# Zeros in place of half-depth score products, in a float32 kernel of one block and two hybrid layers

## The chip, the cores and the metric

One core of a Trainium2 chip runs the whole kernel. The metric is the time on the device in microseconds; smaller is better. The kernel is one program with its instructions unrolled (39424 of them), on TensorE (PE, its weight loads shown as PEld), VectorE (DVE), ScalarE (ACT), GpSimd (POOL) and SyncE (SP), which issues the transfers.

## The reference

All is float32, 256 latent tokens and 256 context tokens, width 1024. A first block on the latent tokens alone, then two layers on both:

```
first block:  proj = rms_norm(x) @ w_in
  a: 8 query heads of 64 on 2 key/value heads; rms_norm and rotation of q, k
     out_a = softmax(q k^T / 8) v
  b: 8 heads of 64; rms_norm of q, k; three dilated windows, mixed by their
     softmax denominators (here one bias per head and pair of tokens)
  x += [rms_norm(out_a), rms_norm(out_b)] @ w_out
  x += conv_ffn(rms_norm(x))
layer l = 0, 1:  h = rmsnorm(x) * (1 + scale) + shift, latent and context
  attention: 8 heads, each with 2 components c of 64; keys: latent and context
     s_c = q_c k_c^T / 8;  p_c = softmax(s_c);  o = (p_0 - lam * p_1) v
  state space part (32 heads of 64, 8 groups, both directions), gates, merge, MLP
out = rmsnorm(x)
```

The context's own outputs are wanted in layer 0 only, so layer 1 has 256 query tokens and layer 0 has 512. The key products of a head's component contract over 64 numbers, and the array has 128 rows.

## The kernel before, in words

**Products.** Most products of the kernel are made of three: an operand is split into a high part (rounded by a copy to float32r, on ACT) and a low part (the rest, on DVE), and high x high, high x low, low x high are summed in PSUM. Weights come in 1 MB loads on SP into three `raw` buffers and are split there (`wload`, L118; `wsplit`, L127). All PE work goes through `mmul` (L315) and `transpose` (L309), so nearly all of it has line L316 or L311 in the profile and is told apart by tile names.

**Order.** While `self.pin` is set, PE keeps the order in which the program emits its instructions. Order on DVE, ACT, POOL and SP is the planner's, from its own costs. A `Stream` (L90) is a generator of products whose work is put out a few columns at a time between the stages of an attention.

**First block (`block1`, L387).** `products` (L486) makes q and k of four heads token-major; `turn4` (L496) transposes them on PE into a PSUM tile `ptq` and ACT copies them to `Tqa`, `Tqb`, `Tka`, `Tkb` (L504 without, L506 with a scale). Each such tile holds two heads on its two halves of 64 partitions; `Tka` has each of its two heads twice (L543). `scores` (L557) takes one head: its 64 partitions of q and of k, one float32 product for each of two query tiles, which the profile shows as two passes each: four of 256 columns per head, 16 heads. Softmax follows on DVE and ACT, `turn` transposes, `weigh` multiplies with v. At each of 18 steps the stream puts products between these three stages. The context `xc` is loaded at L766, after the first block's attention in the program, and is used from `mix_h(0, xc, 1, ...)` (L818) on; the tile itself is allocated for the whole first block.

**Layers (`attention`, L1014).** `qk_g` (L1065) makes q and k of a head h ahead of its scores. For each component c, `qhl[c]` holds q's high part on c's own half of the partitions and its low part on the other; `khh[c]` holds k's high part on both halves; `klo` holds k's low parts, component c's on its own half. A score unit is one head and a group of query tiles (128 tokens each): groups [0], [1], [2, 3] in layer 0 and [0], [1] in layer 1 (L1114). For each component and tile, `scores` (L1117) runs two float32r products into one PSUM region: all 128 rows of `qhl[c]` with `khh[c]` (high x high and low x high at once), then the 64 rows of c's half with `klo` (L1133). Groups of one tile have 512 columns (all keys), the group [2, 3] 256. Between the stages of a unit the stream puts 4096 columns of other products, those of the next head's q, k, v, or gates (`fill_g`, which borrows the tiles tagged khh, klo and qhl at the end).

Of the kernel before, what the change touches and what calls it, by code (L numbers as in the profile page):

```python
# [22 lines left out]
P = 128  # L23
# [40 lines left out]
# a head's columns with the pairs of the rotation in its two halves  # L64
ROPE1 = np.arange(64).reshape(2, 2, 16).transpose(1, 0, 2).reshape(-1)

# how the first products' operands are cut into loads
CUTS = [slice(a, b) for a, b in ((0, 2), (2, 4), (4, 6), (6, 8))]
# columns of products (in 256) between the stages of the first attention
B1_STEP = [7] * 12 + [2.8] * 6  # L70
# the rows of a product at which a stage that waits for the tensor engine comes in
FL = (4, 6)
# steps of the first up products before the norm's sums, and between these and their use
U0, U1 = 6, 4
# the row of the norm's output behind which the up products' next work is put
AF_K = 5
# the first pieces of the first layer's modulation come under the attention, the next ones at these up products
NADA = 4
ADA_UP = (8, 10, 12, 15, 18)
# when the stages of dt's part come in the attention  # L80
DT_STEP = (1, 3, 4, 5, 6, 7, 8)
# independent products between the heads of the attention and between the groups of the state space part, by layer
# [7 lines left out]
class Stream:  # L90
    """Products emitted a few at a time among other work."""
# [13 lines left out]
class Build:  # L105
# [35 lines left out]
    def wloadB(self, src, pool, bufs):  # L141
        """wload for mmB: all 256 columns in one tile"""
        nc = self.nc
        raw = self.wraw.tile([P, 8, 256], F32, tag="raw", name="raw")
        nc.sync.dma_start(raw, src)
        hi = pool.tile([P, 8, 256], F32R, tag="whB", name="whB", bufs=bufs)
        lo = pool.tile([P, 8, 256], F32R, tag="wlB", name="wlB", bufs=bufs)
        for ks in (slice(0, 4), slice(4, 8)):
            self.split(hi[:, ks], lo[:, ks], raw[:, ks])
        return hi, lo  # L150
# [12 lines left out]
    def mm2_g(self, outs, w, x, tok, k0=0, start=True, stop=True):  # L163
        """two products, row by row, in one bank or two"""
# [19 lines left out]
    def mmH_g(self, out, w, m, x, segs, **kw):  # L184
        """mmA, one accumulation per token segment"""
        for t in segs:
            yield from self.mmA_g(out[:, t], w, m, x, t, **kw)
# [40 lines left out]
    def fnorm(self, src, kts, n, dim, pool):  # L228
        """rstd of the mean over features, on all partitions (PSUM): src(k) is [P, n]."""
# [11 lines left out]
    def rstd(self, accs, n, dim, pool, between=None):  # L241
        """1 / sqrt(column sums of all of accs [P, n] / dim + eps), on all partitions (PSUM)"""
# [15 lines left out]
        # Newton's y (3 - v y^2) / 2 without the factors of 2: y grows by -2, 16, -8192  # L258
# [30 lines left out]
    # ------------------------------------------------------------------  # L289
# [30 lines left out]
    # ------------------------------------------------------------------  # L320
# [28 lines left out]
    def ada_g(self, l, j, pool, psum, pend=None, raws=()):  # L349
        """Columns 512 j .. 512 j + 511 of layer l."""  # L350
# [27 lines left out]
    def modcoef(self, l, which, g, col):  # L378
        """g * (1 + scale), for modulation `which` (scale tiles), stream col."""
# [6 lines left out]
    # ------------------------------------------------------------------  # L386
    def block1(self, xl, xc):  # L387
# [4 lines left out]
        with ExitStack() as es:  # L392
# [7 lines left out]
            # the first products' operands come in two halves of the rows  # L400
# [7 lines left out]
            # one start for the bank: it clears what tells the first products from the later ones in all of it  # L408
# [13 lines left out]
            # 1 / rms of each token: kept aside, for it cancels out in the norms of the heads but for their eps  # L422
# [7 lines left out]
            # rope tables times gains  # L430
# [16 lines left out]
            qT = {nm: wa.tile([P, n, S], F32, name="T" + nm) for nm, n in (("qa", 4), ("qb", 4), ("kb", 4), ("ka", 2))}  # L447
# [9 lines left out]
            def b4(ap, n):  # L457
                """[P, t, 64] for n heads"""
                return ap.rearrange("p t (o d) -> p t o d", o=1).broadcast_to([P, 2, n, ap.shape[2]])

            def h64(ap):
                """[P, t, h] for 64 columns"""
# [3 lines left out]
            def hstat(ps, n):  # L466
                """1 / rms of the heads of token-major products [P, t, n, 64], over that of the token"""
# [28 lines left out]
            def turn4(y, dst, scale=None):  # L496
                """token-major [P, t, 256] to [P, i, tokens]"""
# [5 lines left out]
                if scale is None:  # L503
                    nc.scalar.copy(dst, p3)  # L504
                else:
                    nc.scalar.activation(out=dst, in_=p3, func=AF.Identity, scale=scale)  # L506
# [3 lines left out]
            def qk_g(ci, nm, q):  # L510
# [12 lines left out]
                def later():  # L523
                    turn4(y.rearrange("p t h d -> p t (h d)"), qT[nm][:, 2 * q:2 * q + 2, :],
                          None if nm == "qa" else self.v1(nm + "c"))
# [10 lines left out]
            def kv():  # L536
# [9 lines left out]
                pend.append(lambda: turn4(yd.rearrange("p t b i d -> p t (b i d)"), qT["ka"]))  # L546

            # mixed = [norm(a), norm(b)]
# [8 lines left out]
            def scores(grp, h):  # L557
                j, rows = h // 2, slice(64 * (h % 2), 64 * (h % 2) + 64)
                q_, k_ = (qT["qa"][rows, j, :], qT["ka"][rows, h // 4, :]) if grp == "a" else (qT["qb"][rows, j, :], qT["kb"][rows, j, :])
# [187 lines left out]
            # the first two chunks start before the norm, which is made good after their products  # L747
# [13 lines left out]
        # conv ffn  # L761
# [80 lines left out]
    # ------------------------------------------------------------------  # L842
    def modulated(self, wk, x, t0, A, B, hi, lo):
        """hi/lo[:, k, t0:t0 + 256] = rmsnorm(x) * A + B"""
# [16 lines left out]
    def settle(self, x2, c, accs, tile, xa=None, A=None):  # L861
        """the squares of two new residual tiles, summed, and the tiles times A"""
# [22 lines left out]
    def apply(self, xa, r, B, h, t0):  # L885
        """h[:, k, t0:t0 + 256] = xa * r + B, split"""
# [8 lines left out]
    def mmdt_g(self, out, w, x, t):  # L895
        """64 columns of products: w's high and low parts side by side, their products on the two halves of the partitions"""
# [10 lines left out]
    def lead_w(self, l, w):  # L907
        """the weights of dt's products"""
# [5 lines left out]
    def lead(self, l, h, accs, xa, ads, wd):  # L914
        """the norm ahead of layer l on the latent tokens, with the context's part of the first products meanwhile"""
# [32 lines left out]
    def dt_g(self, l, ps, rows, lat_only):  # L948
        """the step sizes, token-major, and what hangs on them alone; rows: bias and log of a on all partitions"""
# [16 lines left out]
        # softplus: max(v, 0) + log(1 + exp(-|v|)), the logarithm as 2 artanh(e / (2 + e))  # L966
# [41 lines left out]
        if lat_only:  # L1008
            # only the states that leave the context are asked for: its first chunk's weights reach to its end
# [3 lines left out]
    # ------------------------------------------------------------------  # L1013
    def attention(self, l, hx, NQ, psd, psk, psq, wq):  # L1014
# [4 lines left out]
        with ExitStack() as es:  # L1019
            wk = es.enter_context(self.pool("att", reuse="tile"))  # L1020
            # lambda
# [33 lines left out]
            def v_g(p, t2s):  # L1055
                """V of heads 2 p, 2 p + 1, token-major"""
# [8 lines left out]
            def qk_g(h):  # L1065
                w = self.wload(a["w_qk"][l, h]) if h else wq
                # per component c: q as its high and low parts on the two halves of the partitions (high on c's
                # own half), k's high part on both halves, k's low part on c's own half
                khh = [wk.tile([P, 512], F32R, tag=f"khh{c}", name="khh", bufs=2) for c in range(2)]
                klo = wk.tile([P, 512], F32R, tag="klo", name="klo", bufs=2)  # L1070
                qhl = [wk.tile([P, NQ], F32R, tag=f"qhl{c}", name="qhl", bufs=2) for c in range(2)]

                def put_k(src, t):
                    for c in range(2):
                        for o in (c, 1 - c):
                            nc.scalar.copy(khh[c][half(o), t], src[half(c)])
                        nc.vector.tensor_tensor(out=klo[half(c), t], in0=src[half(c)], in1=khh[c][half(c), t].bitcast(F32), op=SUB)
# [27 lines left out]
            def products():  # L1105
# [4 lines left out]
                for job, tags in zip(PLAN[l][0], 3 * (("khh0", "khh1"), ("klo", "qhl0"))):  # L1110
# [6 lines left out]
            def scores(h, us):  # L1117
# [8 lines left out]
                for c in range(2):  # L1126
# [3 lines left out]
                    for i, u in enumerate(us):  # L1130
                        o, qs, kt = ps[:, i * kw:(i + 1) * kw], slice(u * 128, (u + 1) * 128), slice(512 - kw, 512)
                        self.mmul(o, qhl[c][:, qs], khh[c][:, kt], start=True, stop=False)
                        self.mmul(o, qhl[c][half(c), qs], klo[half(c), kt], start=False, stop=True)  # L1133
# [102 lines left out]
    # ------------------------------------------------------------------  # L1236
    def att_out_g(self, l, hx, att, NQ, c, wk, saved):
        """2 sigmoid(ga) * (att @ w_attn_o), columns 256 c .. 256 c + 255, to DRAM"""
# [22 lines left out]
    def rows(self, d, c, m, NQ):  # L1261
        """what one tile of 512 columns holds of chunk c in DRAM"""
# [5 lines left out]
    def gate_g(self, l, g, hx, NQ, c, wk, tags, ths, dst):  # L1268
        """2 sigmoid - 1 of columns 256 c .. 256 c + 255 of gate g"""
# [15 lines left out]
    def fill_g(self, l, jobs, hx, att, NQ, wk, tags=("th", "th")):  # L1285
        """products that do not hang on the work around them"""
# [6 lines left out]
    # ------------------------------------------------------------------  # L1293
    def ssd(self, l, hx, NQ, att):
# [6 lines left out]
        with ExitStack() as es:  # L1301
# [5 lines left out]
            def conv(ps, n, ti, dst):  # L1307
                """half of the 5-tap convolution + bias, then silu; n tokens in segments of 256"""
# [52 lines left out]
            def products(g, us):  # L1361
# [4 lines left out]
                if g == 7:  # L1366
                    # the merge's first products, as far as ys has come
# [6 lines left out]
            for g in range(8):  # L1374
# [8 lines left out]
                # token-major B and x  # L1383
# [30 lines left out]
                # states entering each chunk  # L1414
# [28 lines left out]
                def decay(c):  # L1443
                    """the weights of chunk c's tokens on its outputs, and of the state entering it"""
# [7 lines left out]
                    # forward decay below the diagonal, backward above it: the other exponent is 0 there  # L1452
# [18 lines left out]
                def output(c, E, R):  # L1471
                    """outputs of chunk c: [P, j, tokens]; those of two chunks in one bank where there are no others"""
# [61 lines left out]
                if g == 7:  # L1534
                    # more of them for the time in which the last ys come
# [24 lines left out]
    def so_g(self, l, ys, NQ, c, i, ps=None):  # L1560
        """ys @ w_ssd_o, columns 256 c .. 256 c + 255, second half of the rows first: PSUM tiles, products"""
# [15 lines left out]
    # ------------------------------------------------------------------  # L1577
    def merge_mlp(self, l, hx, ys, NQ, xsrc, es_x, es_op):
        """returns the new residual tiles"""
# [8 lines left out]
        with ExitStack() as es:  # L1588
# [89 lines left out]
            if last:  # L1678
                # the shift as one more token (two columns of it), to be added after the products
# [14 lines left out]
        with ExitStack() as es:  # L1694
# [4 lines left out]
            def hidden(j, t, u):  # L1699
                """the squares of u, split: tokens t of hidden tile j"""  # L1700
# [291 lines left out]
```

## Time and profile before

| | |
|---|---|
| three runs | 2402.43 us median (2401.62 to 2403.8) |
| profiled execution: span from its first to its last instruction | 2398.5 us |
| its time beside the span | not given on the page; the median of the runs is 3.9 us above the span |
| mean granted clock of PE | 0.997 |
| busy: PE, DVE, ACT, POOL | 2346.9, 1755.9, 1336.2, 38.4 us |
| chain that ended last | PE 85%, DVE 7%, ACT 5%, DMA 2% |
| first block's attention | about 36 to 128 us |
| attention of layer 0, of layer 1 | about 395 to 640 us, 1640 to 1820 us |

How to read it: a busy share is the union of an engine's instructions. PE's instructions overlap, each lasting longer than the distance to the next, so the distance between starts, not the duration, is what a product takes of the time. In the rows below, `64*128` is the part of the array in rows and columns, `64x512` the moving operand.

### The profile page before, as it was taken

Reading aid. Unit: us, or ns where it says so; the run is one execution under the profiler, and the core shown is the slowest. Engines: PE = TensorE matmul, PEld = TensorE weight load, DVE = VectorE, ACT = ScalarE, POOL = GpSimd, SP = SyncE. Lnnn points to the kernel's source line nnn. Section 1 sums busy time; section 2 is a strip of 40 time slices with the busy share of each in tenths; the row PEclk is TensorE's granted clock in tenths of the full one; section 3 lists DMA queues with packets and bytes.
Section 4 is the critical chain, followed back from the end, with each engine's and each line's share of the span. In section 5 each row is a group of like instructions: output and inputs, shape, how many; then the busy total and the mean of one; then the engine's idle time right before and its main releaser. Section 6 shows DMA issues by size and latency. Waiting matters only on the chain.

```text
span 2398.5 us, 39424 instructions
## 1 busy us (share of the span) xinstructions
PE 2346.9 (98%) x15516; PEld 2027.1 (85%) x15516; DVE 1755.9 (73%) x3562; ACT 1336.2 (56%) x2657; POOL 38.4 (2%) x32
## 2 busy tenths in 40 slices
PE   8999999999999999999999999999999999999998
PEld 7789998787778887778898878798888888899998
DVE  6578766776588878997574334387877999977776
ACT  5556545666466556874334232246776676755553
POOL 1000000000000000000000000000000000000000
PEclk9999999999999999999999999999999999999999
DMA  7546674121334434336334453353224444365553
GB/s 287 174 163 255 225 255 151 56 71 36 112 103 137 132 116 136 116 117 224 110 124 158 158 222 129 123 180 127 91 78 156 137 150 148 113 219 180 186 183 106
DMA packets 75032, 356.57 MB, mean 149 GB/s; under 512 B 9184, under 2 KB 16352, under 8 KB 38368
## 3 DMA queue, kind: packets, MB, share of 16 engines
q1 hardware_dynamic: 71088, 349.31, 42.0%
q10 hardware_dynamic: 3760, 4.75, 0.6%
q8 instruction: 122, 2.00, 0.3%
q14 instruction: 62, 0.51, 0.1%
HBM read 340.15 MB, written 13.89 MB: 148 GB/s over the span
## 4 chain that ended last, share of the span: by engine, by line
PE 85%; DVE 7%; ACT 5%; DMA 2%; issue 1%; SPq 0%; POOL 0%; DVEq 0%; ACTq 0%
PE psm L316 22%; PE psxs L316 6%; PE psso L316 5%; PE psu L316 5%; PE psz L316 4%; PE psk L316 3%; PE psv L316 3%; PE pss L316 3%; PE psga L316 3%; PE psd L316 3%; PE psgs L316 2%; PE pso L316 2%; PE psao L316 2%; PE psB L316 2%; PE psy L316 2%; PE psq L316 2%
## 5 line engine op out<-in xcount | busy, mean ns | idle before, releaser
L136 ACT CAST whi<-raw 128x1024 fp32r<-128x1024 f32 (+1 forms) x430 | 445.3, 1043 | 555.1 <-PE psm L316 263.8
L137 DVE TENSOR_TENSOR wlo<-raw,whi 128x1024 fp32r<-128x1024 f32 (+1 forms) x430 | 522.0, 1218 | 217.4 <-ACT whi L136 212.9
L316 PE MATMUL psm<-dh,whi 128*128 128x256 f32 (+1 forms) x576 | 182.4, 317 | 0.5 <-DVE x L1755 0.5
L316 PE MATMUL psm<-dl,whi 128*128 128x256 f32 (+1 forms) x576 | 182.2, 316 | 0.0
L316 PE MATMUL psm<-dh,wlo 128*128 128x256 f32 (+1 forms) x576 | 182.1, 316 | 0.0
L316 PE MATMUL psm<-hhi,whi 128*128 128x258 f32 (+2 forms) x544 | 179.5, 330 | 1.7 <-ACT whi L136 1.2
L316 PE MATMUL psm<-hlo,whi 128*128 128x258 f32 (+2 forms) x544 | 179.0, 329 | 0.4 <-DVE hlo L893 0.3
L316 PE MATMUL psm<-hhi,wlo 128*128 128x258 f32 (+2 forms) x544 | 178.1, 327 | 0.8 <-DVE wlo L137 0.8
L1456 ACT ACTIVATE E<-R,cstok 128x128 f32<-128x128 f32 x384 | 120.1, 391 | 37.4 <-PE psy L316 28.8
L316 PEld LDWEIGHTS psm<-dh,whi 128*128 128x128 f32 x576 | 108.7, 189 | 9.4 <-issue 1.9
L316 PEld LDWEIGHTS psm<-hhi,whi 128*128 128x128 f32 x544 | 103.1, 190 | 15.1 <-issue 2.9
L316 PEld LDWEIGHTS psm<-dl,whi 128*128 128x128 f32 x576 | 108.6, 189 | 7.4
L316 PEld LDWEIGHTS psm<-dh,wlo 128*128 128x128 f32 x576 | 108.6, 189 | 7.3
L316 PE MATMUL psxs<-hhi,whi 128*128 128x512 f32 x256 | 113.1, 442 | 0.0
L1755 DVE SCALAR_TENSOR_TENSOR x<-psm,mod,x 128x256 f32<-128x256 f32 x96 | 44.1, 481 | 92.2 <-PE psm L316 92.1
L316 PEld LDWEIGHTS psm<-hhi,wlo 128*128 128x128 f32 x544 | 103.2, 190 | 9.8 <-DVE wlo L137 1.2
L316 PEld LDWEIGHTS psm<-hlo,whi 128*128 128x128 f32 x544 | 103.2, 190 | 9.3 <-DVE hlo L893 1.2
L316 PE MATMUL psxs<-hhi,wlo 128*128 128x512 f32 x256 | 100.3, 392 | 0.0
L316 PE MATMUL psxs<-hlo,whi 128*128 128x512 f32 x256 | 100.3, 392 | 0.0
L1317 DVE SCALAR_TENSOR_TENSOR xT<-psxs,halfw,xT 128x510 f32<-128x510 f32 (+1 forms) x128 | 94.5, 741 | 0.5 <-ACT xT L1313 0.2
L1137 ACT ACTIVATE pr<-pss,mx 128x512 f32<-128x512 f32 (+1 forms) x96 | 58.5, 614 | 60.4 <-DVE mx L1135 58.6
L316 PE MATMUL psu<-hhi,whi 128*128 128x256 f32 x320 | 91.6, 286 | 0.5 <-ACT hhi L774 0.5
(470 smaller groups left out, 6985.2 us busy)
## 6 DMA issues: line engine op xcount, KB each, us to landing
raw<-in_w_m SPq DMA_DIRECT2D x68, 1024.0 KB, 4.9
araw<-in_ada SPq DMA_DIRECT2D x48, 1024.0 KB, 5.0
R<-csd SPq DMA_DIRECT2D x48, 512.0 KB, 6.2
raw<-in_w_up SPq DMA_DIRECT2D x22, 1024.0 KB, 5.0
raw<-in_w_qk SPq DMA_DIRECT2D x16, 1024.0 KB, 4.9
raw<-in_w_bc SPq DMA_DIRECT2D x16, 1024.0 KB, 5.1
raw<-in_w_xs SPq DMA_DIRECT2D x16, 1024.0 KB, 4.9
raw<-in_w_z SPq DMA_DIRECT2D x16, 1024.0 KB, 5.0
```

The lines of the kernel that those rows point to most:

```text
L136: nc.scalar.copy(h, r)
L137: nc.vector.tensor_tensor(out=lo[:, :nk, :n], in0=r, in1=h.bitcast(F32), op=SUB)
L316: i = self.nc.tensor.matmul(*args, **kw)
L1137: nc.scalar.activation(out=pt_[:, i * kw:(i + 1) * kw], in_=ps[:, i * kw:(i + 1) * kw], func=AF.Exp, scale=0.125, bias=mx[:, i:i + 1], acc ...
L1317: nc.vector.scalar_tensor_tensor(out=y[:, :, lo:hi], in0=u[:, :, lo + o:hi + o], scalar=wj(j), in1=y[:, :, lo:hi], op0=MUL, op1=ADD)
L1456: nc.scalar.activation(out=E[:, d, h, :], in_=R[:, d, h, :], func=AF.Relu, scale=-1.0, bias=self.cs_tok[:, c, i:i + 1])
L1755: nc.vector.scalar_tensor_tensor(out=xs[col][:, k, :], in0=ps[:, t], scalar=self.mod[l][:, 40 + k, col:col + 1], in1=xs[col][:, k, :], op0 ...
```

## The change

All score products become 128 rows deep. In the layers `klo` becomes a tile for each component, whose other half is set to zero on POOL for every head (two memsets of 64x512), and the second product uses all of `qhl[c]` with it: q's part on the other half meets zeros. In the first block the transposed keys get a tile for each half, `Tka0`, `Tka1` and, for b, the two halves of `xc`; the other 64 partitions of each are set to zero once (four memsets), and `turn4` copies each half of the partitions by an instruction of its own. q keeps its tiles. The number of products and their columns stay as they were. The rest of the diff takes out comments.

```diff
-            qT = {nm: wa.tile([P, n, S], ...) for nm, n in (("qa", 4), ("qb", 4), ("kb", 4), ("ka", 2))}
+            qT = {nm: wa.tile([P, n, S], ...) for nm, n in (("qa", 4), ("qb", 4))}
+            kT = {"ka": [wa.tile([P, 2, S], F32, name=f"Tka{i}") for i in range(2)], "kb": [xc[:, 4 * i:4 * i + 4, :] for i in range(2)]}
+            hrow = [slice(0, 64), slice(64, 128)]
+            for ts in kT.values():
+                for i in range(2):
+                    nc.gpsimd.memset(ts[i][hrow[1 - i]], 0.0)
...
-            def turn4(y, dst, scale=None):
+            def turn4(y, dsts, scale=None):
...
+                for rows, dst in dsts:
+                    if scale is None:
+                        nc.scalar.copy(dst[rows], p3[rows])
+                    else:
+                        nc.scalar.activation(out=dst[rows], in_=p3[rows], func=AF.Identity, scale=scale[rows])
...
+                    js = slice(2 * q, 2 * q + 2)
+                    dsts = [(slice(0, P), qT[nm][:, js, :])] if nm in qT else [(hrow[i], kT[nm][i][:, js, :]) for i in range(2)]
...
-                j, rows = h // 2, slice(64 * (h % 2), 64 * (h % 2) + 64)
-                q_, k_ = (qT["qa"][rows, j, :], qT["ka"][rows, h // 4, :]) if grp == "a" else (qT["qb"][rows, j, :], qT["kb"][rows, j, :])
+                j, i = h // 2, h % 2
+                q_, k_ = (qT["qa"][:, j, :], kT["ka"][i][:, h // 4, :]) if grp == "a" else (qT["qb"][:, j, :], kT["kb"][i][:, j, :])
...
-                klo = wk.tile([P, 512], F32R, tag="klo", name="klo", bufs=2)
+                klo = [wk.tile([P, 512], F32R, tag=f"klo{c}", name="klo", bufs=2) for c in range(2)]
+                for c in range(2):
+                    nc.gpsimd.memset(klo[c][half(1 - c)].bitcast(F32), 0.0)
...
-                        self.mmul(o, qhl[c][half(c), qs], klo[half(c), kt], start=False, stop=True)
+                        self.mmul(o, qhl[c][:, qs], klo[c][:, kt], start=False, stop=True)
```

## Rows read from the trace of the kernel before

**Rows 1.** The page: its head, and busy time, share and count of PE.
```profile
span 2398.5 us, 39424 instructions
...
PE 2346.9 (98%) x15516; PEld 2027.1 (85%) x15516; DVE 1755.9 (73%) x3562; ACT 1336.2 (56%) x2657; POOL 38.4 (2%) x32
```

**Rows 2.** Stretches of the two layers' attentions: length, then busy time by engine, clock.
```profile
395.00:640.00 245.00, 240.98 (x1310) 192.00 (x1309) 172.20 (x447) 159.04 (x412) 0.00 (x0) 1.00 0.20 69
1640.00:1820.00 180.00, 180.00 (x1209) 156.37 (x1208) 141.46 (x375) 127.71 (x297) 0.00 (x0) 1.00 0.28 99
```

**Rows 3.** Waits of PE, 395 to 645 us: total, times, longest.
```profile
PE pto L311 <- DVE o L1180: 1.4, 1, 1.4
...
PE pto L311 <- DVE dk L1005: 0.4, 1, 0.4
```

**Rows 4.** Timeline of PE, layer 0, one-tile unit: start us, duration us, instruction.
```profile
581.16 0.39 PE L316 MATMUL psgs<-hhi,wlo 128*128 128x512 f32 x1
581.40 0.40 PE L316 MATMUL pss<-khh,qhl 128*128 128x512 f32 x1
581.72 0.49 PE L316 MATMUL pss<-klo,qhl 64*128 64x512 f32 x1
582.14 0.50 PE L316 MATMUL pss<-khh,qhl 128*128 128x512 f32 x1
...
583.34 0.40 PE L316 MATMUL psgs<-hlo,whi 128*128 128x512 f32 x1
583.57 0.39 PE L316 MATMUL psgs<-hhi,wlo 128*128 128x512 f32 x1
```

**Rows 5.** Groups by line and form, PEld: count, busy us, mean ns, idle before.
```profile
L316 PEld LDWEIGHTS psgs<-hlo,whi 128*128 128x128 f32 x128 | 24.3, 190 | 2.8 <-issue 0.7
```

**Rows 6.** Timeline of PE, layer 0, a unit of two tiles.
```profile
599.75 0.40 PE L316 MATMUL psgs<-hhi,wlo 128*128 128x512 f32 x1
...
602.94 0.39 PE L316 MATMUL psgs<-hhi,wlo 128*128 128x512 f32 x1
```

**Rows 7.** Timeline of PE, layer 1, around a unit.
```profile
1788.77 0.28 PE L316 MATMUL psga<-hhi,wlo 128*128 128x256 f32 x1
...
1790.72 0.28 PE L316 MATMUL psga<-hlo,whi 128*128 128x256 f32 x1
1790.84 0.28 PE L316 MATMUL psga<-hhi,wlo 128*128 128x256 f32 x1
```

**Rows 8.** Timeline of PE, first block, one head.
```profile
43.19 0.28 PE L316 MATMUL psqk<-whB,hlo 128*128 128x256 f32 x1
43.40 1.13 PE L316 MATMUL pss<-Tka,Tqa 64*128 64x256 f32 x4
...
44.68 0.28 PE L316 MATMUL psqk<-wlB,hhi 128*128 128x256 f32 x1
```

**Rows 9.** Timeline of PE, state space part, float32 passes of 128 rows.
```profile
693.08 0.59 PE L316 MATMUL psst<-xw,Bt 128*128 128x256 f32 x2
...
693.75 0.40 PE L316 MATMUL psz<-hlo,whi 128*128 128x512 f32 x1
```

**Rows 10.** Timeline of POOL: the first row and one of the state space part.
```profile
0.24 0.10 POOL L1983 MEMSET const-float32-0.0<- 128x1 f32 x1 [0.24 <-issue]
...
728.46 1.42 POOL L1541 TENSOR_TENSOR ssq<-y 128x512 f32<-128x512 f32 x1 [709.48 <-DVE y L1539]
```

**Rows 11.** Tile Tkb: its copy (ns min/median/max, first and last start), its waiters.
```profile
L506 ACT ACTIVATE Tkb<-ptq,vb x2: 687/687/687, 80.2 to 112.2; 128x512 f32<-128x512 f32 x2
...
  PE pss L316: 1.6, 2
```

**Rows 12.** Tile xc: its load's issue, its first reader, landing of its transfers.
```profile
L766 SPq DMA_DIRECT2D xc<-in_ctx x1: 1133/1133/1133, 44.3 to 44.3; - x1
...
L234 ACT ACTIVATE sqa<-xc x1: 421/421/421, 168.3 to 168.3; 128x256 f32<-128x256 f32 x1
...
DMA to landing us min/median/max: 7.9/8.4/8.9
```

More of the change, by code (lines that the diff above doesn't have):

```diff
@@ L446, in block1 @@
                 tabs[nm] = (gc, gs)
-            qT = {nm: wa.tile([P, n, S], F32, name="T" + nm) for nm, n in (("qa", 4), ("qb", 4), ("kb", 4), ("ka", 2))}
+            qT = {nm: wa.tile([P, n, S], F32, name="T" + nm) for nm, n in (("qa", 4), ("qb", 4))}
+            kT = {"ka": [wa.tile([P, 2, S], F32, name=f"Tka{i}") for i in range(2)], "kb": [xc[:, 4 * i:4 * i + 4, :] for i in range(2)]}
[3 more added lines that the diff above has]
+                    nc.gpsimd.memset(ts[i][hrow[1 - i]], 0.0)
             vA = wa.tile([P, 2, 128], F32, name="vA")
@@ L502, in turn4 @@
                 p3 = pt.rearrange("p (i t) -> p i t", i=2)
[L503 to L506, printed above, removed]
+                for rows, dst in dsts:
[3 more added lines that the diff above has]
+                        nc.scalar.activation(out=dst[rows], in_=p3[rows], func=AF.Identity, scale=scale[rows])
             ready = set()
@@ L523, in later @@
                 def later():
-                    turn4(y.rearrange("p t h d -> p t (h d)"), qT[nm][:, 2 * q:2 * q + 2, :],
-                          None if nm == "qa" else self.v1(nm + "c"))
+                    js = slice(2 * q, 2 * q + 2)
+                    dsts = [(slice(0, P), qT[nm][:, js, :])] if nm in qT else [(hrow[i], kT[nm][i][:, js, :]) for i in range(2)]
+                    turn4(y.rearrange("p t h d -> p t (h d)"), dsts, None if nm == "qa" else self.v1(nm + "c"))
                     ready.add((nm, q))
@@ L545, in kv @@
                     nc.vector.tensor_tensor(out=yd[:, :, :, i, :], in0=y, in1=h64(rs), op=MUL)
-                pend.append(lambda: turn4(yd.rearrange("p t b i d -> p t (b i d)"), qT["ka"]))
+                pend.append(lambda: turn4(yd.rearrange("p t b i d -> p t (b i d)"), [(hrow[i], kT["ka"][i]) for i in range(2)]))
             mix = {"a": [wk.tile([P, 4, S], F32R, name="m" + n) for n in ("hi", "lo")]}
@@ L1076, in put_k @@
                             nc.scalar.copy(khh[c][half(o), t], src[half(c)])
-                        nc.vector.tensor_tensor(out=klo[half(c), t], in0=src[half(c)], in1=khh[c][half(c), t].bitcast(F32), op=SUB)
+                        nc.vector.tensor_tensor(out=klo[c][half(c), t], in0=src[half(c)], in1=khh[c][half(c), t].bitcast(F32), op=SUB)
                 def put_q(src, t):
@@ L1109, in products @@
                         yield from v_g((h + 1) // 2, (h % 2,))
-                for job, tags in zip(PLAN[l][0], 3 * (("khh0", "khh1"), ("klo", "qhl0"))):
+                for job, tags in zip(PLAN[l][0], 3 * (("khh0", "khh1"), ("klo0", "qhl0"))):
                     yield from self.fill_g(l, [job], hx, None, NQ, wk, tags)
```

## The prediction

> **What bounds the kernel now.** I read the page's head and busy table first: the span is 2398.5 us and TensorE (PE) is busy 98% of it [rows 1]. A busy PE need not be a PE at its peak, so next came the table of stretches for the two attentions of the second block: in 395 to 640 us PE is busy 240.98 of 245 us, in 1640 to 1820 us 180.00 of 180, at a granted clock of 1.00 (2.4 GHz), while VectorE (DVE) has 172.20 of 245 and 141.46 of 180 and GpSimd (POOL) nothing at all [rows 2]. The waits of PE in the first stretch are four, from 1.4 to 0.4 us, 4.0 in all [rows 3]; in the second the waits view lists none. So here the order of PE's instructions, which is pinned, sets the end, and what one instruction adds to the distance between starts is added to the span. That is why I then left busy times and means (the 0.49 us of a 512-column klo product [rows 4] are its latency, and overlap its neighbour) and went to the timeline of PE alone, where starts can be subtracted.
>
> **What the 64-row products cost.** In a plain stream of 128-row products with 512 columns, starts are 0.23 us apart (583.34 to 583.57), with a weight load of 190 ns for each, hidden [rows 4, 5]. Around a score unit they are not. Take a unit of one query tile: psgs starts at 581.16, then khh, klo, khh, klo, psgs, and the second psgs after the unit starts at 583.34, the third at 583.57. From 581.16 to 583.57 are seven steps; at 0.23 they take 1.61 us, and they take 2.41. So 0.80 us of a unit is neither streaming nor waiting for data. The excess sits at the changes between 128 and 64 rows: klo to khh takes 0.42 (582.14 less 581.72) where 0.23 would do, and the first klo after khh 0.32. A unit of two query tiles has eight products of 256 columns, so eight changes: 599.75 to 602.94 is 3.19 us; three steps at 0.23 and eight at 0.12 make 1.65; the excess is 1.54 [rows 6]. The 0.12 is the step of 256 columns in the same 128-row stream, 1790.72 to 1790.84. The unit in the second layer, 1788.77 to 1790.84, takes 2.07 against 0.12 + 4 x 0.23 + 2 x 0.12 = 1.28, an excess of 0.79 [rows 7]. The first block's scores are float32 with both products 64 rows deep, so they change only on entering and on leaving: 43.19 to 44.68 is 1.49 us for one 256-column product ahead, four passes, and one product behind [rows 8]. A 128-row float32 pass of 256 columns takes 0.22: two of them and a 512-column product take 693.08 to 693.75, 0.67, less 0.23, halved [rows 9]. So 0.12 + 4 x 0.22 + 0.12 = 1.12 would do, and the excess is 0.37. Also, four 64-row passes within a unit stay about as dense as 128-row ones, so rows as such cost nothing; the changes do.
>
> The Trainium skill, "TensorEngine Tiling (Array Packing)", Key Properties, says that changing the tiling mode, not just the tile, drains the engine. The trace agrees with it at each of these steps. The same page's Performance Considerations advise row tiling where the contracted dimension is 64 or less, which speaks for the kernel before; it pays only where products of different row halves run side by side, and in rows 8 the four passes of one unit lie one behind another.
>
> **The change part by part.** (a) klo products and the first block's scores become 128 rows deep. Count of units from the code: first layer 8 heads x 2 single and 8 double, second layer 8 heads x 2 single, first block 16. Removed: 16 x 0.80 + 8 x 1.54 = 25.1; 16 x 0.79 = 12.6; 16 x 0.37 = 5.9; sum 43.6. Taken off: six units are followed by dt's transposes and 32-column products, where part of the change stays (estimate from the same steps, 1.0), and in the first block four units border on 32-column psada products and three start after an idle PE, where only about half is freed (estimate 1.0). Left: 41.6 us. The number of products, their columns and the number of weight loads stay the same.
>
> (b) Two memsets of 64x512 per head on POOL, 32 in all, and four before the first attention. No such row exists. Bounds: a 128x1 memset takes 0.10, a 128x512 two-operand operation 1.42 [rows 10]. I take about 0.7, between the two. POOL is empty in all three stretches, each head's klo buffer was last read two heads earlier (at 9 to 11 us a unit, over 20 us before), and nothing queues behind a memset on POOL there. What waits for it is the first klo product, which sits in PE's queue with everything behind it; it needs DVE's klo anyway, written later than a memset that waits for nothing. So zero, with 2.8 us per head (two at the upper row, exposed in full) as the far end; below zero is excluded, since it only adds an instruction. In DVE's idle (73 and 39 us) a shared delay of 22 us would fit.
>
> (c) The transposed keys are copied out of PSUM in two 64-row pieces. One 128x512 ACT copy with a scale takes 0.687 us; a piece has as many columns, so I take the same again, three times in all, and PE already waits for this copy twice, 1.6 us [rows 11]. Even heads need only the first piece, so the cost is between 0 and 1.4; I take 0.7.
>
> (d) The second half of the first attention's keys now lives in xc, which the context is loaded into. Now that load is issued on the SP queue at 44.3 us and first used at 168.3; it will have to wait until the last kb product, about 125 us, and on SP the loads of w_up queue behind it. With the longest landing of these transfers, 8.9 us, it is there by 134 and 34 us early [rows 12]. I take 0; at most the w_up loads slip by the few us that a plan made for another time is off, say 4.
>
> (e) What is late next. Waits of PE that end on DVE or ACT have a chain that doesn't get shorter: 4.0 us in the first layer's attention and at least 1.6 in the first block's [rows 3, 11]. As units shrink by 8% some of it grows; I give back 2.0. DVE in the second layer goes from 141.46 of 180 to the same of 167, 85%: full, but its results are used a unit (10 us) later.
>
> Sum: 41.6 - 0.7 - 2.0 = 38.9. The profiled span 2398.5 becomes 2359.6. The page gives no time beside the span; the three runs have a median of 2402.43, 3.9 above it, and with that added the forecast is 2363 us.
>
> **Rivals.** *The load of weights stays exposed.* The excess of a step (0.42 less 0.23) is just one weight load (0.19) [rows 4, 5], so it could be that khh and klo of one unit, sharing rows, cannot load under each other. Then each product takes 0.19 + 0.23 = 0.42 as today, and the time is 2402. Against it: 128-row streams with a new load for each product run at 0.23 and 0.12 [rows 4, 7]. The Trainium skill, "TensorE: Matmul & The Clock Gate", Part 3, says that weight loads overlap running products only when the row group differs, and by that nothing is won. The trace disagrees with it wherever 128-row products follow each other. Chance 4%.
>
> *DVE becomes the bound in the second layer.* 85% busy, with chains through ACT; were the 12.6 us there and 2 us at the start of the state space part lost, the time would be 2378. For it: DVE's share; against: no PE wait at all in that stretch [rows 2]. Chance 10%.
>
> *The memsets stand in PE's way.* If the planner puts them so late that the first klo product of a head waits for both, 16 heads x 2.8 us = 45 us come in and 38.9 go out: 2402 + 6 = 2408, slower. It turns from a gain at 2.4 us exposed per head. Against it: the buffer is free more than 20 us before and POOL is empty. Chance 4%.
>
> **How the numbers follow.** Forecast 82%, with 2357 to 2370 as its own range. To hold 8 in 10 with the second rival and a shifted plan on DVE, ACT and SP, the range is 2353 to 2383; the low end is the full 43.6 and some 6 us of luck in the plan. A difference under 0.2% (5 us) can't be told from none here: faster 0.93, same 0.03 (most of the first rival), slower 0.04.
>
> **What would show it.** In the changed timeline: khh and klo at 0.23 and 0.12 from start to start, first psgs after a unit not followed by 0.34; single units 0.8 us and double ones 1.5 us closer; first layer's attention about 24 us shorter, the second's 12, the first block's 4 to 5; POOL some 36 memsets, and none of them named in a wait of PE; the context's load after 125 us with no wait on xc. Wrong if steps between khh and klo stay at 0.4, if PE in the second layer shows waits on DVE, or if PE waits for klo ends on POOL.

## The result and the profile after

The changed kernel takes 2376.22 us (median of 4 runs, 2373.3 to 2378.92) against 2403.11 for the kernel before, timed beside it (4 runs, 2401.62 to 2403.93): ratio 0.9895, interval 0.9883 to 0.9907. It is faster, as forecast, by 25 us by the ratio or 27 by the medians, where 39 was forecast: 13 us above the forecast, inside the range. The profile is that of the slowest of the four runs (2378.92 us, span 2377.1; the four spans have a median of 2374.4), so it holds some 3 us more of loss than the middle run. The page, whose rows answer to [rows 1]:

```profile
span 2377.1 us, 39531 instructions
PE 2315.6 (97%) x15516; PEld 2033.6 (86%) x15516; DVE 1753.3 (74%) x3562; ACT 1337.1 (56%) x2660; POOL 57.9 (2%) x68
```

PE has as many products as before, POOL 36 instructions more. PE's busy share fell from 98% to 97%: some of the time taken out of PE's queue came back as waiting.

**The score units.** The timeline of PE around the same one-tile unit of layer 0 as in [rows 4] (start, duration, instruction), and behind it, cut to the ends, the units of [rows 6] and [rows 7]:

```profile
570.55 0.39 PE L316 MATMUL psgs<-hhi,wlo 128*128 128x512 f32 x1
570.77 0.40 PE L316 MATMUL pss<-khh,qhl 128*128 128x512 f32 x1
571.01 0.40 PE L316 MATMUL pss<-klo,qhl 128*128 128x512 f32 x1
571.24 0.40 PE L316 MATMUL pss<-khh,qhl 128*128 128x512 f32 x1
571.48 0.39 PE L316 MATMUL pss<-klo,qhl 128*128 128x512 f32 x1
571.71 0.39 PE L316 MATMUL psgs<-hhi,whi 128*128 128x512 f32 x1
571.94 0.40 PE L316 MATMUL psgs<-hlo,whi 128*128 128x512 f32 x1
572.17 0.40 PE L316 MATMUL psgs<-hhi,wlo 128*128 128x512 f32 x1
...
587.51 0.39 PE L316 MATMUL psgs<-hhi,wlo 128*128 128x512 f32 x1
...
589.15 0.40 PE L316 MATMUL psgs<-hhi,wlo 128*128 128x512 f32 x1
...
1769.12 0.28 PE L316 MATMUL psga<-hhi,wlo 128*128 128x256 f32 x1
...
1770.40 0.28 PE L316 MATMUL psga<-hhi,wlo 128*128 128x256 f32 x1
```

Seven steps now take 1.62 us (570.55 to 572.17) instead of 2.41; the unit of two tiles takes 1.64 instead of 3.19 [rows 6], the one of layer 1 1.28 instead of 2.07 [rows 7]. The steps of the one-tile unit are 0.22 to 0.24 throughout: the mark of the change from 128 to 64 rows is gone. In the first block, the timeline of PE that answers to [rows 8] has 1.11 us from the product ahead to the product behind, instead of 1.49:

```profile
43.05 0.28 PE L316 MATMUL psqk<-whB,hlo 128*128 128x256 f32 x1
...
44.16 0.28 PE L316 MATMUL psqk<-wlB,hhi 128*128 128x256 f32 x1
```

Summed over all 24 units of layer 0, what the starts show beyond plain streaming falls from 24.6 us to 0.9; over the 16 of layer 1 from 12.2 to 0.5. The first block's 16 units, read as in the pair above, are 4.5 us shorter.

**Where the rest went.** PE runs the same 15516 products in the same order in both traces, so the start of each can be subtracted from its start before. The lead of the changed kernel, which is that difference, is 4.1 us when layer 0's attention begins, 16.8 at its end, 16.1 when layer 1's attention begins, 22.0 at its end and 21.0 at the end of the program. Layer 0's attention freed 23.7 and kept 12.7; layer 1's freed 11.7 and kept 5.9. The waits of PE in the two stretches (total us, times, longest), first layer 0, 390 to 632 us, which answers to [rows 3], then layer 1, 1615 to 1800:

```profile
PE pto L311 <- DVE o L1191: 5.8, 3, 3.4
PE pto L311 <- DVE dk L1014: 2.2, 1, 2.2
PE ptp L311 <- DVE dve L974: 1.8, 1, 1.8
PE psv L316 <- DVE klo L1088: 1.2, 1, 1.2
...
PE pto L311 <- DVE o L1191: 2.9, 1, 2.9
```

With a shorter one on ACT (0.3) these are 11.3 us in layer 0 against 4.0 before, and 2.9 in layer 1 against none (one of 0.3 on wlB, ahead of the first scores, is in both kernels). That is 7.3 of the 11.0 lost in layer 0 (23.7 less 12.7) and 2.9 of the 5.8 lost in layer 1. The rest goes with the clock. The stretches of the two attentions, which answer to [rows 2], and then short stretches around the waits (length, busy time of PE, PEld, DVE, ACT, POOL, granted clock, DMA share, GB/s):

```profile
390.00:632.00 242.00, 230.73 (x1358) 200.62 (x1358) 175.62 (x466) 162.97 (x426) 6.26 (x12) 0.98 0.21 72
1615.00:1800.00 185.00, 181.78 (x1294) 169.85 (x1292) 147.34 (x391) 136.28 (x313) 8.34 (x16) 0.98 0.29 99
...
445.00:449.00 4.00, 0.59 (x5) 0.39 (x4) 3.47 (x12) 1.27 (x6) 0.00 (x0) 0.81 0.13 53
449.00:454.00 5.00, 5.00 (x19) 4.42 (x18) 4.02 (x9) 4.00 (x9) 0.00 (x0) 0.50 0.00 0
511.00:514.00 3.00, 3.00 (x17) 2.62 (x18) 2.06 (x5) 2.52 (x9) 0.00 (x0) 0.72 0.28 49
514.00:518.00 4.00, 4.00 (x18) 3.21 (x17) 3.04 (x6) 3.27 (x7) 0.00 (x0) 0.78 0.54 225
1677.00:1684.00 7.00, 6.88 (x36) 6.88 (x37) 5.19 (x13) 6.57 (x17) 0.00 (x0) 0.56 0.32 132
1829.00:1835.00 6.00, 5.51 (x33) 5.48 (x34) 4.46 (x9) 2.34 (x4) 0.00 (x0) 0.72 0.00 0
```

From 449 to 454 us PE is busy all 5 us at a granted clock of 0.50, its lower level of 1.2 GHz, and so does work worth 2.5. By the length of each such stretch times the share of the clock that is missing, they cost 2.5 + 3 x 0.28 + 4 x 0.22 = 4.2 us in layer 0 and 7 x 0.44 = 3.1 in layer 1. Waits and clock make 11.5 and 6.0; the loss by the starts is 11.0 and 5.8. The stretch 1829 to 1835, already in layer 1's state space part, is worth 6 x 0.28 = 1.7; the lead loses 1.5 there (from 22.0 to 20.5).

**Why PE waits there.** At the end of each head DVE writes the normalized output o, and PE, whose order is pinned, stands at the transposes pto until it comes. The timeline of PE in the changed kernel (in brackets the idle time before and what ended it):

```profile
436.38 1.05 PE L316 MATMUL po<-V,pT 128*128 128x128 f32 x8
...
445.00 0.28 PE L316 MATMUL psv<-whB,hlo 128*128 128x256 f32 x1
448.69 1.11 PE L311 MATMUL pto<-cons,o 128*128 128x128 f32 x4 [3.41 <-DVE o L1191]
...
451.73 0.63 PE L316 MATMUL psk<-hlo,whi 128*128 128x512 f32 x1
452.16 0.63 PE L316 MATMUL psk<-hhi,wlo 128*128 128x512 f32 x1
```

And of DVE, in the same stretch:

```profile
441.27 0.16 DVE L1187 TENSOR_SCALAR ss<-ss 128x4 f32<-128x4 f32 x1
...
444.32 0.43 DVE L1093 TENSOR_TENSOR qhl<-psq,qhl 64x256 fp32r<-64x256 f32 x1
444.97 0.42 DVE L1093 TENSOR_TENSOR qhl<-rot,qhl 64x256 fp32r<-64x256 f32 x1
...
447.94 0.69 DVE L1191 TENSOR_TENSOR o<-po,nwy 128x512 f32<-128x512 f32 x1
```

The same places in the kernel before, PE:

```profile
444.36 1.05 PE L316 MATMUL po<-V,pT 128*128 128x128 f32 x8
...
456.15 0.66 PE L311 MATMUL pto<-cons,o 128*128 128x128 f32 x4 [1.37 <-DVE o L1180]
```

and DVE:

```profile
448.75 0.16 DVE L1176 TENSOR_SCALAR ss<-ss 128x4 f32<-128x4 f32 x1
...
455.41 0.69 DVE L1180 TENSOR_TENSOR o<-po,nwy 128x512 f32<-128x512 f32 x1
```

From the first operation on ss to the start of o it is 6.67 us now (441.27 to 447.94) and was 6.66 (448.75 to 455.41): DVE runs, nearly without a gap, a chain of small steps for the norm's root, and between these, in turn, the rotation and the subtractions (qhl) of the next head's queries and the maxima (mx) of its scores. PE's own work from po until it stands at pto shrank from 10.4 us (444.36 to 456.15, less 1.37) to 8.9 (436.38 to 448.69, less 3.41), DVE's did not, and the wait grew from 1.37 to 3.41. (From po to the start of o it is even 0.5 longer, 11.56 against 11.05: DVE comes to ss later behind po.) Not every head waits. In layer 0 it is the first and the third, whose o ends 12.3 and 10.9 us after po starts, while PE needs 8.9 and 8.8; from the fourth to the seventh o ends after 6.5 to 8.7 and PE comes after 8.5 to 8.8. The wait of 2.9 in layer 1 is of the same make: from the split wlo ahead of the first head's norm to the start of o DVE takes 13.73 us (1662.92 to 1676.65) and took 13.72 before (1679.81 to 1693.53), with the same operations. Behind the wait of 3.41 the step of two 512-column products is 0.43 (451.73 to 452.16) where 0.23 is usual: the lower clock again.

### The profile page after: what moved, and what is told of

It is laid out like the page before. It is cut to its first block, busy times and chain, and to the rows that moved or that the text cites. A ratio compares the mean times of both kernels' runs of the same rounds, so it can differ in the third digit from the quotient of the medians.

```text
span 2377.1 us, 39531 instructions
## 1 busy us (share of the span) xinstructions
PE 2315.6 (97%) x15516; PEld 2033.6 (86%) x15516; DVE 1753.3 (74%) x3562; ACT 1337.1 (56%) x2660; POOL 57.9 (2%) x68
## 4 chain that ended last, share of the span: by engine, by line
PE 81%; DVE 9%; ACT 6%; DMA 2%; issue 1%; SPq 0%; POOL 0%; DVEq 0%; ACTq 0%; POOLq 0%
PE psm L316 21%; PE psxs L316 6%; PE psso L316 6%; PE psu L316 5%; PE psz L316 4%; PE psk L316 3%; PE psga L316 3%; PE psd L316 3%; PE psgs L316 2%; PE pso L316 2%; PE psv L316 2%; PE psao L316 2%; PE psB L316 2%; PE psy L316 2%; PE po L316 2%; PE psada L316 2%
```

## The experiments

Each was timed beside the kernel before, whose median moved between 2399.7 and 2403.1 from one group of runs to the next, so ratios are compared. The changed kernel itself stands at 0.9895 [0.9883, 0.9907].

**The two parts by themselves.** One kernel has the change in the layers' attentions alone, the other in the first block alone.

> The kernel before with the change in the two layers alone (klo in two tiles with zeros); the first block's scores stay 64 rows deep. By the shift of PE's starts in the trace (4.1 us by the end of the first block's attention, 21.0 in all) about 2403 - 22 = 2381. If the parts hinder each other (the xc load, the plan of the other engines), their sum differs from the whole by over 3 us.

> The kernel before with the change in the first block alone (Tka in two tiles, kb in xc). Both theories: 4 to 5 us faster, about 2399. If the late load of xc or the copy in two pieces costs something, less than 3 us faster.

Measured: 2380.01 us, 0.9914 [0.99, 0.9928], and 2396.66 us, 0.9988 [0.9979, 0.9996]. The product of the two ratios is 0.9902, within the interval of the whole: the parts add up as far as these runs can tell. The layers give about 20.6 us where the forecast had 36.7 freed; this is where the loss is. The first block gives 3 us by medians, where 4 to 5 were expected, and a lead of 4.4 behind its attention in its trace.

**Give the wait more to cover it: head output later.** The transposes pto and what follows are moved behind the next stage of the head's pipeline.

```diff
-                if done is not None:
-                    headout(*done)
-                    done = None
+                out, done = done, None
...
                 bg.run(step)
+                if out is not None:
+                    headout(*out)
```

> The changed kernel with headout (the transposes pto of a head's result) put out one stage of the stream, 4096 columns or 1.8 us, later. Theory A: the change freed about 41 us of PE, and some 14 of it came back because PE now reaches pto of the early heads before DVE has its input (3.4, 2.2 and 2.1 us in layer 0, 2.9 in layer 1), with up to 6 us at half clock behind the waits of about 3 us. Then 1.8 us more room takes these waits to 1.6 or less, no stretch falls to the lower clock, and the time is 2376 less 4 x 1.8 less some 5 of clock: about 2364. Rival B: DVE as a whole is behind in the early heads, and the wait only moves to the next instruction of PE that needs DVE: 2374 to 2377.

The same edit on the kernel before:

> The kernel before with headout one stage later. Theory A: before the change PE waits for pto 1.4 and 0.4 us in all and no clock falls there, so the later place gives about 2 us: 2401. Rival C: the later place is worth something by itself, whatever the score products do (as much as it gives the changed kernel, 8 us or more): 2395 or less.

Measured: 2374.33 us, 0.9894 [0.988, 0.9907], no different from the changed kernel; and 2401.86 us, 1.0007 [0.9998, 1.0016] on the kernel before, where about 2 us were expected and none came. The waits of PE, 390 to 632 us, in the changed kernel with pto later:

```profile
PE po L316 <- DVE o L1191: 4.2, 2, 3.5
PE po L316 <- DVE mx L1146: 2.2, 1, 2.2
```

The wait has only changed its owner. The next head's po goes into the one PSUM buffer that o still reads, so it stands where pto stood, for 3.5 us. Theory A was missed and rival B came true: the place of the consumer is not the cause, the time at which DVE delivers o is.

**Is it the load of dt's part on DVE?** The stages of dt, which fall on the first heads, are spread over the attention.

```diff
-DT_STEP = (1, 3, 4, 5, 6, 7, 8)
+DT_STEP = (1, 4, 6, 8, 10, 12, 14)
```

> The changed kernel with the stages of dt's part at units 1, 4, 6, 8, 10, 12, 14 in place of 1, 3, 4, 5, 6, 7, 8. Theory B1 (after the run with a later headout, where the wait on DVE's o only moved on to po): DVE's work for dt, about ten operations of 0.42 us packed into units 3 to 8, delays the result o of the early heads. Then the waits on o (3.4 and 2.1 us in layer 0, 2.9 in layer 1) fall under 1.5 us, no stretch runs at half clock, and the time is about 2366. Theory B2: the order of DVE's own operations within a head (the small steps of the head's norm stand between those of the next head's q) sets it: the 3.4 and 2.9 stay, 2373 to 2377.

Measured: 2377.68 us, 0.9907 [0.9892, 0.9922]. The wait of the first head in layer 0 stays at 3.40 us, and all its waits on o grow from 5.8 to 8.1, while the one of 2.2 on dk goes; in layer 1 the one of 2.9 at the first head goes, those of 0.7 and 1.0 on o come at the next two, and one of 3.0 at 1761 us. For layer 0 this reason falls.

**Is it the order on DVE?** The norm of the head's output is given a high priority with the scheduler.

```diff
+                with self.tc.high_priority():
                     ss = wk.tile([P, 4], F32, tag="ss", name="ss", bufs=2)
...
```

> The changed kernel with the head's norm (squares on ACT, 13 small DVE operations, the product o) at high priority in the plan, so that DVE and ACT take it ahead of the next head's q and k. Theory B2: from the first small step to o's end are 7.4 us in the trace for 3.4 us of work; with the norm first o is ready 3 to 4 us sooner, the waits of 3.4 and 2.9 us go, no half clock: about 2365. Theory B1 (dt's load): o is late by the load ahead of it, under 1 us better: 2374 to 2377. Either may lose some where k or q of the next head comes later.

Measured: 2374.43 us, 0.9888 [0.9873, 0.9903]. The timeline of DVE in this kernel, in layer 0:

```profile
439.95 0.16 DVE L1188 TENSOR_SCALAR ss<-ss 128x4 f32<-128x4 f32 x1
...
446.60 0.69 DVE L1192 TENSOR_TENSOR o<-po,nwy 128x512 f32<-128x512 f32 x1
```

and of PE:

```profile
447.35 1.12 PE L311 MATMUL pto<-cons,o 128*128 128x128 f32 x4 [3.40 <-DVE o L1192]
```

It is 6.65 us again, with the same instructions in between: the priority did not reorder DVE here, so for layer 0 the experiment says nothing. In layer 1 the wait on o fell from 2.9 to 0.3, and one of 2.0 on dk came.

**What the clock costs by itself.** Eight float32 products of a constant, some 1.95 us, go ahead of the first head's pto, into the buffer that pto then overwrites.

```diff
+                if h == 0:
+                    for _ in range(8):
+                        self.mmul(pb[:, :128], self.one1, self.one1, start=True, stop=True)
```

> The changed kernel with eight float32 products of constants (about 1.7 us, their result overwritten) ahead of the first head's pto in both layers, where PE waits 3.4 and 2.9 us. Theory: the granted clock of 0.50 to 0.6 behind these two waits (about 5 us each time) comes from PE having idled; with half of each wait filled the clock stays at 1.00, no wait is made longer, and the time falls by 2.5 to 5 us, to 2371 to 2374. Rival: the clock has another cause, or the filler counts for nothing: 2376, or 2379 if the filler simply adds its time.

Stretches of this kernel around the wait, which is now 1.61 us instead of 3.41:

```profile
445.00:449.00 4.00, 2.39 (x22) 2.20 (x21) 3.57 (x13) 1.28 (x6) 0.00 (x0) 1.00 0.16 66
449.00:454.00 5.00, 5.00 (x31) 4.33 (x31) 3.93 (x9) 4.52 (x11) 0.00 (x0) 1.00 0.00 0
```

In the same 5 us PE ran 31 instructions at clock 1.00 instead of 19 at 0.50, and stood 2.45 us ahead of the changed kernel just behind it. So at this place the low clock belongs to the idle time, not to the work behind it, and costs its 2.5 us on top of the wait. All six traces here with a wait of 3.4 to 3.7 us at this place have the lower clock behind it. The whole was missed: 2376.19 us, 0.9894 [0.9879, 0.9908]. The profiled run was 3.2 us shorter in span (2373.9), which is no more than the four runs of the changed kernel differ among themselves (2371.5 to 2377.1); it has a new slow stretch (clock 0.63) at 1719 to 1723 behind a wait on dk of 1.98, and the medians show no gain.

**The memsets.** Each runs twice.

> The changed kernel with each of the 32 memsets of klo done twice. If they are free, as the prediction took them to be: 2376, within 1.5 us. If POOL's writes hold up DVE or ACT and so are part of what was given back: slower by as much as one set costs, 3 us or more.

Measured: 2378.86 us, 0.9901 [0.9884, 0.9917], with nearly the same waits in layer 0 as the changed kernel (6.0 on o, 2.6 on dk, 1.8 on dve) and none on POOL. Their cost can't be told from zero.

**Relieve DVE.** Four of a head's subtractions, those on the rotated part, go to POOL, which is nearly idle.

```diff
-    nc.vector.tensor_tensor(out=klo[c][half(c), t], ..., op=SUB)
+    (nc.gpsimd if t == lat else nc.vector).tensor_tensor(out=klo[c][half(c), t], ..., op=SUB)
...
-    nc.vector.tensor_tensor(out=qhl[c][half(1 - c), t], ..., op=SUB)
+    (nc.gpsimd if t == lat else nc.vector).tensor_tensor(out=qhl[c][half(1 - c), t], ..., op=SUB)
```

> The changed kernel with four subtractions per head that read SBUF (low parts of the rotated k and q, 64x256, 0.42 us each on DVE) on POOL, which is idle there. Theory: in the early heads the span of DVE's and ACT's work from a head's products to its result o has become the bound, 7.4 us of it DVE without a gap; with 1.7 us of DVE work per head gone from it, the waits on o (3.4, 2.1, 2.9 us) shrink by 1 to 2 us each, fewer stretches at half clock: 2366 to 2371. Rival: DVE is not what they wait for in the end (a fixed chain through ACT, or the dt part): 2375 to 2378; slower still if POOL, about 1 us for such an operation, brings q or k too late.

The same on the kernel before, as a control:

> The kernel before with the same four subtractions per head on POOL (64-row klo products). Theory: DVE is not the bound while the score products take their 0.8 to 1.5 us more per unit, so at most the 1.4 us wait on o goes: 2399 to 2402. Rival: POOL's relief is worth as much here as in the changed kernel (5 us or more).

Measured: 2369.82 us, 0.9872 [0.9858, 0.9885], as expected; and 2402.24 us, 1.0007 [0.9998, 1.0016] on the kernel before. The first interval just meets that of the changed kernel (from 0.9883 on), and the two were not timed side by side, so the gain of some 5 us on it is likely and not certain; what the edit does to the wait is read from the trace. The timeline of PE in the changed kernel with the subtractions on POOL, at the same place as above:

```profile
435.52 1.05 PE L316 MATMUL po<-V,pT 128*128 128x128 f32 x8
...
446.65 0.66 PE L311 MATMUL pto<-cons,o 128*128 128x128 f32 x4 [2.24 <-DVE o L1192]
```

and of DVE:

```profile
445.90 0.69 DVE L1192 TENSOR_TENSOR o<-po,nwy 128x512 f32<-128x512 f32 x1
```

Its waits of PE, first 390 to 632 us, then 1600 to 1800:

```profile
PE pto L311 <- DVE o L1192: 3.2, 3, 2.2
...
PE pss L316 <- POOL qhl L1094: 2.7, 1, 2.7
```

From po to the start of o it is 10.38 us (435.52 to 445.90) instead of 11.56 (436.38 to 447.94), and the wait falls by the same, from 3.41 to 2.24. All waits of layer 0's attention fall from 11.3 to 7.2, and the stretches 511 to 518 and 1677 to 1684 are back at clock 1.00. Two of the four subtractions that stood between the steps of the root are gone from DVE's queue, and in layer 0 no edit before this one made DVE's time between po and o shorter (11.5 to 11.8 us in the traces of all of them). On the kernel before, the edit takes 2.8 us of waits off layer 0 (4.0 to 1.2), puts one of 2.0 on POOL's qhl into layer 1, with clock 0.57 in 1669 to 1673, and gains nothing in time. So this control does not show by itself that relief pays only once PE is shorter. In layer 1 of the changed kernel POOL's subtraction, 0.77 us a piece against 0.42 on DVE, is late itself, and PE waits 2.7 for it.

**All three together, and each where it helps.** First the late head output, the priority and POOL's subtractions in both layers; then POOL and the late output in layer 0 alone, the priority in layer 1 alone.

> The run with subtractions on POOL, the head's norm at high priority and headout one stage later together. Theory: as before, and what is left of the waits falls into the later place: 2362 to 2368, the best of all. Rival: each wait only moves on to the next consumer, 2373 or more.

> The changed kernel with what each layer's trace liked best: in layer 0 the four subtractions on POOL and headout one stage later, in layer 1 the norm at high priority and headout in its old place. If the stretches add up as the shifts of PE's starts in the single runs say (first block 4, layer 0 22, layer 1 and behind it 9 us), the span is 35 us below the kernel before: 2365 to 2368, faster than the changed kernel by some 8 us. If each relief changes what the next layer's plan does, 2370 to 2374.

Measured: 2372.88 us, 0.989 [0.9876, 0.9903], a miss: layer 1 had new waits, 3.5 on alo and 2.7 on POOL's qhl. By layer: 2368.31 us, 0.9866 [0.985, 0.9883], the fastest of all, with waits on o down to 3.4 in layer 0 (5.8 in the changed kernel). Its interval and that of the changed kernel meet at 0.9883, so it is likely some 7 us better than the changed kernel (0.0029 of 2401), though the two were not timed side by side; against the kernel before it gains some 32, where 35 were expected.

## Why the prediction was right, and where it was not

**(a) Changes between 128 and 64 rows: right.** 41.6 us were to be freed; the starts show 23.7 in layer 0, 11.7 in layer 1 (35.4 where 36.7 was worked out) and 4.5 in the first block (where 4.9 was): 39.9. The Trainium skill, "TensorEngine Tiling (Array Packing)", Key Properties, says that a change of tiling mode drains the engine; the excess of 0.8 us a one-tile unit, gone with the mode, agrees.

**(b) Memsets: right, at no price.** Two of 64x512 take 1.09 us on POOL, 0.55 each where 0.7 was estimated; none is named in a wait of PE, and doubling them changed nothing that can be measured.

**(c) Key copies: hidden.** There are four of 0.682 us, and PE's wait for them is 1.5 us as it was 1.6 [rows 11]. The 0.7 set down for them was not needed.

**(d) The context's load: right.** Tile xc of the changed kernel (issue, landing):

```profile
L775 SPq DMA_DIRECT2D xc<-in_ctx x1: 327/327/327, 121.5 to 121.5; - x1
...
DMA to landing us min/median/max: 3.8/5.4/6.9
```

Issued at 121.5, it is there by 128.4, 36 us before its reader at 164.2.

**(e) What is late next: the step that failed.** "As units shrink by 8% some of it grows; I give back 2.0": in the profile it is 18.3 us (11.0 in layer 0, 5.8 in layer 1, 1.5 behind it), which leaves a lead of 21 of the 39.9 freed; by the ratio and the medians, with 25 to 27 gained, some 13 to 15 came back. Two things were mis-sized. The waits of PE in the two attentions grew by 7.3 and 2.9, since DVE's part of a head stayed and PE's shrank: at the first head the wait grew by 2.0 where PE's stretch lost 1.5. And that DVE's "results are used a unit (10 us) later", said of the second layer, is no cover for o: in layer 0 its chain from po on takes 12.25 us (436.38 to the end of o at 448.63), longer than PE's 8.9 between. What was not in the sum at all is the clock: behind some of the waits of 2 to 3.4 us PE ran at 0.50 to 0.78, worth 7.3 us in the two attentions and 1.7 behind them. In the attentions of the two layers the trace of before, with a longest wait of 1.4 and clock 1.00 [rows 2, 3], had no such row. But it had one in the first block's attention:

```profile
80.00:128.00 48.00, 44.36 (x334) 35.38 (x333) 30.49 (x77) 25.55 (x64) 0.00 (x0) 0.96 0.49 170
```

The missing 0.04 lies in 99 to 103 us (clock 0.57), behind a wait of 1.6 for oa. So before the change the trace already showed that a short wait can cost the clock as well.

**The 3.9 us beside the span.** It is too much. In every run with both on record the time is 1.7 to 2.2 us above the span, so the profile of before came from a faster execution than the three runs timed; with 2 us the forecast would have been 2361.6.

**The rivals.** *The load of weights stays exposed*: fallen, khh to klo is 0.24 from start to start. "TensorE: Matmul & The Clock Gate", Part 3, of the Trainium skill, with its overlap only between different row groups, is contradicted once more: each of these 128-row products has a load of its own. *DVE becomes the bound in the second layer* (2378): its time came nearly true, but with some luck, and its place only in part. The prediction's own mark, a wait on DVE in layer 1, did appear (2.9 us, and 5.8 lost of 11.7 there), but the greater loss lies in layer 0. That 2376 lies inside the range is owed to this rival and to the room for a shifted plan, for whose sake the range went up to 2383. The mechanism deserved more than its 10%, and both layers. *The memsets in PE's way*: fallen.

**Open.** Why the priority moved nothing on DVE in layer 0 wasn't found. How much of the loss is waits and how much clock is known from one profile of each kernel. Nor was an edit found that takes the waits of both layers at once.

## What to carry to other kernels

Products of another row depth in a stream of full-depth ones cost their change-over (here 0.8 us for a unit of four), and it is read from starts and not from busy times; with zeros on the idle partitions nearly all of it went (24.6 to 0.9 us in layer 0), the zeros being written by an engine that was idle. When an engine with a pinned order gets shorter in a stretch, take each place where it uses another engine's result: how long it works from handing over the input to needing the result, less the shortening, against how long the other engine takes between these two points. See whether the other engine has idle time *in its queue between them*, not over the whole stretch. Then look in the trace of before for stretches at the lower clock behind waits, and keep a term for more of them.

## What was not expected of the hardware

The lower clock came in stretches of 3 to 7 us in attentions that are at 1.00 throughout in the kernel before, each behind a wait: 0.50 behind 3.4 us idle, 0.56 behind 2.9. Filling part of the first with products kept 1.00. But the length of the wait alone does not decide: PE waited 2.6 us for xT ahead of the transposes ptx at the same place of layer 1 in both kernels, and in the kernel before the clock stayed at 1.00 behind it (the stretch that answers to 1829 to 1835):

```profile
1851.00:1857.00 6.00, 5.49 (x39) 5.21 (x40) 5.81 (x12) 3.84 (x6) 0.00 (x0) 1.00 0.00 0
```

The same wait also goes both ways from one execution to another. The 2.9 us on o in layer 1 have clock 0.56 behind them in the changed kernel and 1.00 in the kernel with the change in the layers alone (1679 to 1688). The 1.6 to 1.7 us on oa in the first block have 0.57 behind them in the kernel before and in the changed one (95.5 to 99.5), and 1.00 in the kernel with the change in the first block alone. So the price of the clock, read from one profile, is that of one execution. What else decides it, no run here shows.
